# A PSUM tile of its own for each prompt head's scores, and another place for the second gate's weights, in a two-layer hybrid decoder step

## The chip, the cores and the metric

The kernel runs on one core of a Trainium2 chip. The metric is the time of one launch in device microseconds (us), the median of the runs. Engines are named as the profile names them: PE is TensorE's matmul, PEld its weight load, DVE VectorE, ACT ScalarE, POOL GpSimd, SP SyncE, which here only issues DMAs.

## What is computed

Two layers work on a prompt of 256 tokens and on 8 samples of 8 tokens (320 tokens together). Each layer adds to x the output projection of three gated branches: a pooling mixer, latent attention (MLA) and a gated delta rule. One projection of the normalised x feeds all of them and the gates. The change lies in the latent attention of the prompt:

```python
def _mla_attend(q_lat, q_rope, c_kv, k_rope, q_pos, k_pos):
...
        s = (jnp.einsum('bqhc,bkc->bhqk', ql, c_kv, preferred_element_type=jnp.float32)
             + jnp.einsum('bqhr,bkr->bhqk', qr, k_rope, preferred_element_type=jnp.float32)) * MLA_SCALE
        mask = k_pos[None, :] <= qp[:, None]
        p = jax.nn.softmax(jnp.where(mask[None, None], s, -jnp.inf), axis=-1)
        o = jnp.einsum('bhqk,bkc->bqhc', p.astype(c_kv.dtype), c_kv, preferred_element_type=jnp.float32)
```

There are 8 heads. The gates are `sigmoid` of columns of the same input projection and scale each branch's product with its output weights.

## The kernel before

A layer runs in this order: projections with the pooling and the delta rule (a scheduler sets the order of the instructions there, by its own estimate of times), then the **head stage** (latent attention of the prompt, head by head), then the **sample stage** (the 8 samples' attention over 2048 cached tokens each, one sample at a time), then the branch products and the output projection. In the head stage and the sample stage the order on PE, DVE, ACT and POOL is the order in which the code is written (`manual_schedule`); each of these engines does its instructions in that order, and one that waits holds up all behind it.

The head stage is a loop over h = 0 to 10, which has several heads under way at once. In round h:

- **scores** of head h (L1278, L1279): four products on PE into 384 columns of a PSUM bank; `head_max` (L1283, L1284): two maxima on DVE; `head_soften` (L1289, L1290): two exponentials on ACT with their sums;
- for h < 2 the **values** (L1358), 4 products; for h = 4 the POOL queue gets the gather of the second sample's cache;
- a **flip** (L1167, L1164) on DVE: it transposes a quarter of the first sample's keys, or its rotary part, into KT and krT. `flips` says in which round which of the five is done;
- head h - 2 is **turned** (L1301): three transposes on PE into an A tile, copied by ACT to pPT (L1303);
- in rounds 2, 3, 7 and 8 half of a **gate** product (L220 to L222): 12 products on PE;
- `head_scale` (L1294 to L1296): reciprocals of the sums on DVE, then two multiplications on POOL. The turning of the head waits for them;
- head h - 3 is **attended** (L1310, L1311) from pPT and the values; DVE puts the result into zs (L1312).

A gate's weights come by `gate_w`: a load to wraw on the SP queue, ahead by four buffers, then `split_w`, which makes two halves, wh by a copy on ACT (L196) and wl by a subtraction on DVE (L197), which waits for wh. The second gate's `gate_w` stands at the end of round 4, so that DVE meets it ahead of the maxima of head 5 (the sixth head).

The scores of all heads go into one PSUM tile, hsc, of four banks: head h uses the quarter h % 4. The framework follows what reads and writes a tile as a whole: the scores of a head wait for the exponentials of the head before (L1290). The same four banks then hold the sample scores sc (L1177), which round 9 begins; four more, the A tiles, serve the turned heads, the attended heads and the gates. Ahead of this stage the eight banks belong to another pool, in which the last users are the products kn (L1123), copied by ACT (L1125).

Of the kernel before, what the change touches and what calls it, by code (L numbers as in the profile page):

```python
# [11 lines left out]
F32 = mybir.dt.float32  # L12
# [5 lines left out]
PSUM = bass.MemoryType.PSUM  # L18
# [98 lines left out]
def trunk(tc, I, O, layers=2):  # L117
# [3 lines left out]
    pool = lambda name, **k: ctx.enter_context(tc.tile_pool(name=name, bufs=1, **k))  # L121
# [20 lines left out]
    def enter(*a, **k):  # L142
        st = ExitStack()
        return st, st.enter_context(phase(*a, **k))
# [265 lines left out]
    for l in range(layers):  # L410
# [717 lines left out]
        p1c.close()  # L1128
        kvp = p2c.enter_context(tc.tile_pool(name=f"kv_{l}", bufs=1, side="right", reuse_waits="tile"))
        olat = p2.tile([128, 2, 8, 64], F32, tag="qlat", name="olat", bufs=1)  # L1130
        p2b, pa = enter(f"pa_{l}", dict(A=4, S=1), "right")
        pdc, phc, pbc = ExitStack(), ExitStack(), ExitStack()
        pd = pdc.enter_context(tc.tile_pool(name=f"pd_{l}", bufs=1, reuse_waits="tile"))

        def load_wuv(t):
# [33 lines left out]
        def scores(keys, q4):  # L1169

            KT, krT = keys
            sc = banks["pool"].tile([128, 4, 512], F32, tag="S", name="sc", bufs=1)
            for k in range(9):
                for hf in range(2):
                    for g in range(4):
                        r, keys_ = slice(32 * g, 32 * g + 32), slice(256 * hf, 256 * hf + 256)
                        nc.tensor.matmul(  # L1177
                            sc[64 * hf : 64 * hf + 64, g, :256], q4[r, k, :], krT[r, keys_] if k == 8 else KT[r, k, keys_],
                            start=k == 0, stop=k == 8,
                        )  # L1180
            return sc
# [160 lines left out]
        with tc.manual_schedule(engines={mybir.EngineType.PE, mybir.EngineType.DVE, mybir.EngineType.Activation, mybir.EngineType.Pool}):  # L1342
            ph = phc.enter_context(tc.tile_pool(name=f"ph_{l}", bufs=1, side="right", reuse_waits="tile"))
            wuv = load_wuv(ph.tile([128, 1024], F32, name="wuv"))
            vv = ph.tile([128, 2, 512], F32, name="vv")

            im = ph.tile([128, 2, 128], F32R, name="im")
            act(im[:, 0], ident, AF.Copy)
            act(im[:, 1], c("causal")[:, :128], AF.Copy)
            gather(0)  # L1350
            q4 = load_q(0)
            nm, w = gate_w()
            hsc = banks["pool"].tile([128, 4, 512], F32, tag="S", name="hsc", bufs=1)

            def values(t):
                b = ps("A", "vv")
                for cc in range(2):
                    nc.tensor.matmul(b, ckv[:, cc, t * 128 : t * 128 + 128], wuv[:, cc, :], start=cc == 0, stop=cc == 1)  # L1358
                act(vv[:, t, :], b, AF.Copy)


            keys = key_tiles()
            flips = {3: 0, 4: 1, 5: 2, 6: 3, 7: 4}
            hs, hp = {}, {}
            b = sc = None
            for h in range(11):
                if h < 8:
                    head_scores(h, hsc[:, h % 4])
                    st2 = head_max(hsc[:, h % 4])
                    hs[h] = head_soften(hsc[:, h % 4], st2), st2  # L1370
                if h < 2:
                    values(h)
                if h == 4:
                    gather(1)
                if h in flips:
                    flip(0, keys, flips[h])
                if h - 2 in hs:
                    hp[h - 2] = head_turned(hs[h - 2][0])
                if h in (2, 3):
                    b = gate_mm("A", w, b, (4 * (h - 2), 4 * (h - 2) + 4))  # L1380
                if h in (7, 8):
                    b = gate_mm("A", w, b, (4 * (h - 7), 4 * (h - 7) + 4))
                if h in hs:
                    head_scale(*hs[h])
                if h - 3 in hs:
                    head_attend(h - 3, hp[h - 3])
                if h == 3:
                    gate_out(nm, b, True)
                    b = None
                if h == 4:  # L1390
                    nm, w = gate_w()
                if h == 8:
                    gate_out(nm, b, True)
                    pair[0] = paired[0] = 1
                    gs = [gate_w() for _ in range(GL[0])]
                if h == 9:
                    sc = scores(keys, q4)
            phc.close()
            pb = pbc.enter_context(tc.tile_pool(name=f"pb_{l}", bufs=1, side="right", reuse_waits="tile"))
            q4 = load_q(1)  # L1400
            mx = stats(0)
            o = None
            for bb in range(NB):
                more = bb + 1 < NB
                S = soften(bb, sc, mx)
                if more:
                    keys = key_tiles()
                    flip(bb + 1, keys, 0)
                    nmx = stats(bb + 1)
                softened(bb, S, mx)  # L1410
                if more:
                    flip(bb + 1, keys, 1)
                g = [(gs[0][0], gate_mm("A", gs[0][1]))]
                if o is not None:
                    ob = combine(o)
                    combined(bb - 1, ob)
                gate_out(*g[0], bb < 6)
                if more:
                    flip(bb + 1, keys, 4)
                    flip(bb + 1, keys, 2)  # L1420
                two = len(gs) > 1
                if two:
                    b = gate_mm("A", gs[1][1], ks=(0, 4))
                PT = turned_p(S)
                PTn = turned_own(bb)
                if two:
                    gate_mm("A", gs[1][1], b, (4, 8))
                    gate_out(gs[1][0], b, bb < 6)
                weigh(bb, mx)
                o = attend(bb, PT, PTn, mx)  # L1430
                if more:
                    flip(bb + 1, keys, 3)
                    gs = [gate_w() for _ in range(GL[bb + 1])]
                    sc = scores(keys, q4)
                    mx = nmx
                    if bb + 2 < NB:
                        q4 = load_q(bb + 2)
            wuv = load_wuv(pb.tile([128, 1024], F32, tag="S", name="wuv", bufs=2))
            pdc.close()
            p3e = ExitStack()  # L1440
            p3a = p3e.enter_context(tc.tile_pool(name=f"p3a_{l}", bufs=1, reuse_waits="tile"))
            yb = {}
            split_y(p3a, 0)
# [10 lines left out]
                    nc.tensor.matmul(b[64 * e : 64 * e + 64, p * 64 : p * 64 + 64], wuv[:, cc, h * 64 : h * 64 + 64], olat[:, cc, h, :], start=cc == 0, stop=cc == 1)  # L1454
        for p in range(4):
            stt(zs[4 + p][:, TP:], b[:, p * 64 : p * 64 + 64], 0.5, zs[4 + p][:, TP:], mult, mult)
        pbc.close()
        p2b.close()
        p2c.close()
# [90 lines left out]
```

## Time and profile before

| | |
|---|---|
| median of 3 runs | 1057.81 us (1056.7 to 1057.89) |
| profiled execution | 1062.18 us |
| its span | 1060.1 us |
| mean granted clock of PE in it | 0.968 |
| PE busy | 995.1 us, 94% of the span |
| DVE busy | 708.6 us, 67% |
| ACT busy | 465.0 us, 44% |
| POOL busy | 329.5 us, 31% |

The span is what the profile shows of the launch; the profiled execution is 4.4 us longer than the median. The granted clock is a share of TensorE's full speed: at 1 it runs at 2.4 GHz, at 0.5 at 1.2 GHz. "Busy" counts neither DMA issue nor waiting. PE is the engine that is busy most, so what matters is where PE waits, for whom, and where it runs at the lower clock.

### The profile page before, as it was taken

The numbers are of one execution on the slowest core, as the hardware profiler recorded it, in microseconds if no ns is written. First come the engines' busy times: TensorE is split into PE (matmuls) and PEld (weight loads), VectorE is DVE, ScalarE is ACT, GpSimd is POOL, SyncE is SP. The second block draws the span as 40 slices with busy tenths as digits, with TensorE's granted clock in tenths as the row PEclk, the third lists the DMA queues.
The fourth block names the chain that finished last, engine by engine and source line by source line (L and its number), as shares of the span: only waits on it lengthen the run. The fifth ranks groups of instructions, "written<-read, shape, count | busy, mean of one in ns | idle before, by whom it ended". The sixth has DMA issues, their size and how long they took to land. (4 is left out here: it accounts for less than half of the span.)

```text
span 1060.1 us, 24775 instructions
## 1 busy us (share of the span) xinstructions
PE 995.1 (94%) x10211; PEld 869.1 (82%) x10211; DVE 708.6 (67%) x1353; ACT 465.0 (44%) x838; POOL 329.5 (31%) x467
## 2 busy tenths in 40 slices
PE   8989899999989999989989978989999999999996
PEld 6877798887878887779978867979887778777996
DVE  3899984558556666568659878645674657674872
ACT  5554353454543333344546624326445333334453
POOL 3566321215240101035345542212234211000631
PEclk7999999999989999999999979999999999999998
DMA  8533333633746776258563322345264477742861
GB/s 232 154 81 99 100 84 91 182 96 113 211 131 191 245 232 228 79 166 249 141 200 82 99 80 72 99 133 133 81 161 156 150 255 220 248 156 86 262 177 50
DMA packets 202698, 159.22 MB, mean 150 GB/s; under 512 B 27704, under 2 KB 191826, under 8 KB 200010
## 3 DMA queue, kind: packets, MB, share of 16 engines
q1 hardware_dynamic: 176364, 98.47, 34.3%
q0 software_dynamic: 7424, 48.75, 12.8%
q10 hardware_dynamic: 18798, 10.44, 3.4%
q8 instruction: 80, 1.31, 0.5%
q14 instruction: 32, 0.26, 0.1%
HBM read 144.17 MB, written 13.68 MB: 149 GB/s over the span
## 5 line engine op out<-in xcount | busy, mean ns | idle before, releaser
L197 DVE TENSOR_TENSOR wl<-wraw,wh 128x1024 fp32r<-128x1024 f32 (+2 forms) x169 | 195.2, 1164 | 80.3 <-ACT wh L196 79.6
L196 ACT ACTIVATE wh<-wraw 128x1024 fp32r<-128x1024 f32 (+1 forms) x180 | 166.2, 935 | 165.2 <-PE pj L221 77.8
L220 PE MATMUL pj<-xnH,wh 128*128 128x320 f32 (+1 forms) x528 | 175.4, 332 | 16.9 <-DVE V L497 6.1
L222 PE MATMUL pj<-xnH,wl 128*128 128x320 f32 (+1 forms) x528 | 172.4, 327 | 7.4 <-DVE wl L197 7.1
L221 PE MATMUL pj<-xnL,wh 128*128 128x320 f32 (+1 forms) x528 | 170.7, 323 | 0.0
L220 PE MATMUL gate<-xnH,wh 128*128 128x320 f32 x384 | 125.1, 326 | 1.7 <-DVE V L497 1.5
L220 PEld LDWEIGHTS pj<-xnH,wh 128*128 128x128 f32 (+1 forms) x528 | 103.8, 197 | 23.3 <-ACT wh L196 8.3
L222 PE MATMUL gate<-xnH,wl 128*128 128x320 f32 x384 | 120.5, 314 | 1.6 <-DVE wl L197 1.3
L221 PE MATMUL gate<-xnL,wh 128*128 128x320 f32 x384 | 119.7, 312 | 0.0
L222 PEld LDWEIGHTS pj<-xnH,wl 128*128 128x128 f32 (+1 forms) x528 | 103.5, 196 | 11.8 <-DVE wl L197 9.1
L221 PEld LDWEIGHTS pj<-xnL,wh 128*128 128x128 f32 (+1 forms) x528 | 103.7, 196 | 5.2 <-issue 3.8
L220 PEld LDWEIGHTS gate<-xnH,wh 128*128 128x128 f32 x384 | 72.9, 190 | 9.3 <-issue 5.7
L1167 DVE STREAM_TRANSPOSE KT<-kv 128x1024 f32<-128x1024 f32 x64 | 78.6, 1228 | 0.4
L222 PEld LDWEIGHTS gate<-xnH,wl 128*128 128x128 f32 x384 | 72.7, 189 | 3.0 <-DVE wl L197 1.8
L221 PEld LDWEIGHTS gate<-xnL,wh 128*128 128x128 f32 x384 | 73.0, 190 | 1.0 <-issue 0.8
L220 PE MATMUL br<-yH,wh 128*128 128x320 f32 x192 | 59.7, 314 | 5.2 <-ACT wh L196 3.3
L1248 PE MATMUL pv<-kv,PT 128*64 128x256 f32 x512 | 58.8, 382 | 2.3 <-ACT PT L1226 2.3
L1177 PE MATMUL sc<-KT,q 32*64 32x256 f32 x2048 | 59.3, 377 | 0.0
L221 PE MATMUL br<-yL,wh 128*128 128x320 f32 x192 | 59.1, 309 | 0.0
L222 PE MATMUL br<-yH,wl 128*128 128x320 f32 x192 | 58.4, 309 | 0.0
L505 DVE SCALAR_TENSOR_TENSOR cy<-V,prm,cy 128x344 f32<-128x344 f32 x72 | 56.4, 803 | 0.5
L1177 PEld LDWEIGHTS sc<-KT,q 32*64 32x64 f32 x2048 | 45.8, 131 | 12.0 <-issue 5.7
(410 smaller groups left out, 2046.8 us busy)
## 6 DMA issues: line engine op xcount, KB each, us to landing
wraw<-in_w_in SPq DMA_DIRECT2D x114, 512.0 KB
wraw<-in_w_out SPq DMA_DIRECT2D x16, 512.0 KB
q<-q4d SPq DMA_DIRECT2D x64, 72.0 KB
gate<-gt ACTq DMA_DIRECT2D x28, 160.0 KB
gt<-gate POOLq DMA_DIRECT2D x28, 160.0 KB, 3.7
wraw<-in_w_br_pool SPq DMA_DIRECT2D x16, 256.0 KB
wraw<-in_w_br_dn SPq DMA_DIRECT2D x16, 256.0 KB
wraw<-in_w_br_mla SPq DMA_DIRECT2D x16, 256.0 KB
```

The costliest lines, as they stand in the source:

```text
L196: act(h, raw, AF.Copy)
L197: (nc.gpsimd.tensor_tensor if spare or turn[0] in K["lo"] else tt)(lo, raw, h.bitcast(F32), sub)
L220: nc.tensor.matmul(out, wh[:, k, :], xh[:, first + k, :], start=k == 0, stop=False)
L221: nc.tensor.matmul(out, wh[:, k, :], xl[:, first + k, :], start=False, stop=False)
L222: nc.tensor.matmul(out, wl[:, k, :], xh[:, first + k, :], start=False, stop=k == nk - 1)
L505: stt(y, V[:, j : j + 344], wj(j), y, mult, add)
L1167: nc.vector.transpose(v[:, a], kv[:, a * 1024 : a * 1024 + 1024].rearrange("p (i k c) -> p i k c", i=4, k=8))
L1177: nc.tensor.matmul(sc[64 * hf : 64 * hf + 64, g, :256], q4[r, k, :], krT[r, keys_] if k == 8 else KT[r, k, keys_], start=k == 0, stop=k == 8,)
L1248: nc.tensor.matmul(pv[64 * hf : 64 * hf + 64, :256], PT[:, n * 128 + 64 * hf : n * 128 + 64 * hf + 64], kv[:, r : r + 256], start=n == 0, ...
```

## The change

Each head's scores get a tile of one bank (tag H, four buffers) in a PSUM pool of their own, hp. The pool is closed in round 9, and the sample scores get another, sp, which is closed after the sample stage. The pool pa keeps the A tiles alone. The second gate's `gate_w` moves from the end of round 4 into round 5, behind the maxima and exponentials of head 5. Flips 2, 3 and 4 move from rounds 5, 6 and 7 to rounds 6, 7 and 8.

```diff
--- before.py
+++ after.py
@@ -1128,8 +1128,9 @@
         p1c.close()
         kvp = p2c.enter_context(tc.tile_pool(name=f"kv_{l}", bufs=1, side="right", reuse_waits="tile"))
         olat = p2.tile([128, 2, 8, 64], F32, tag="qlat", name="olat", bufs=1)
-        p2b, pa = enter(f"pa_{l}", dict(A=4, S=1), "right")
-        pdc, phc, pbc = ExitStack(), ExitStack(), ExitStack()
+        p2b, pa = enter(f"pa_{l}", dict(A=4), "right")
+        pdc, phc, pbc, hpc, spc = (ExitStack() for _ in range(5))
+        bank4 = lambda st, name: st.enter_context(tc.tile_pool(name=f"{name}_{l}", bufs=1, space=PSUM, reuse_waits="tile"))
         pd = pdc.enter_context(tc.tile_pool(name=f"pd_{l}", bufs=1, reuse_waits="tile"))
 
         def load_wuv(t):
@@ -1169,7 +1170,7 @@
         def scores(keys, q4):
 
             KT, krT = keys
-            sc = banks["pool"].tile([128, 4, 512], F32, tag="S", name="sc", bufs=1)
+            sc = sp.tile([128, 4, 512], F32, tag="S", name="sc", bufs=1)
             for k in range(9):
                 for hf in range(2):
                     for g in range(4):
@@ -1350,7 +1351,7 @@
             gather(0)
             q4 = load_q(0)
             nm, w = gate_w()
-            hsc = banks["pool"].tile([128, 4, 512], F32, tag="S", name="hsc", bufs=1)
+            hp_ = bank4(hpc, "hp")
 
             def values(t):
                 b = ps("A", "vv")
@@ -1360,18 +1361,21 @@
 
 
             keys = key_tiles()
-            flips = {3: 0, 4: 1, 5: 2, 6: 3, 7: 4}
+            flips = {3: 0, 4: 1, 6: 2, 7: 3, 8: 4}
             hs, hp = {}, {}
             b = sc = None
             for h in range(11):
                 if h < 8:
-                    head_scores(h, hsc[:, h % 4])
-                    st2 = head_max(hsc[:, h % 4])
-                    hs[h] = head_soften(hsc[:, h % 4], st2), st2
+                    hsc = hp_.tile([128, 512], F32, tag="H", name="hsc", bufs=4)
+                    head_scores(h, hsc)
+                    st2 = head_max(hsc)
+                    hs[h] = head_soften(hsc, st2), st2
                 if h < 2:
                     values(h)
                 if h == 4:
                     gather(1)
+                if h == 5:
+                    nm, w = gate_w()
                 if h in flips:
                     flip(0, keys, flips[h])
                 if h - 2 in hs:
@@ -1387,13 +1391,13 @@
                 if h == 3:
                     gate_out(nm, b, True)
                     b = None
-                if h == 4:
-                    nm, w = gate_w()
                 if h == 8:
                     gate_out(nm, b, True)
                     pair[0] = paired[0] = 1
                     gs = [gate_w() for _ in range(GL[0])]
                 if h == 9:
+                    hpc.close()
+                    sp = bank4(spc, "sp")
                     sc = scores(keys, q4)
             phc.close()
             pb = pbc.enter_context(tc.tile_pool(name=f"pb_{l}", bufs=1, side="right", reuse_waits="tile"))
@@ -1454,6 +1458,7 @@
                     nc.tensor.matmul(b[64 * e : 64 * e + 64, p * 64 : p * 64 + 64], wuv[:, cc, h * 64 : h * 64 + 64], olat[:, cc, h, :], start=cc == 0, stop=cc == 1)
         for p in range(4):
             stt(zs[4 + p][:, TP:], b[:, p * 64 : p * 64 + 64], 0.5, zs[4 + p][:, TP:], mult, mult)
+        spc.close()
         pbc.close()
         p2b.close()
         p2c.close()
```

On PE in the head stage of layer 0 these are the rows from head 5's scores to the start of head 6's, with the semaphores that each waits for (named by the engine that raises them); first before, then changed (line numbers are one higher there):

```order
L1278 MATMUL hsc<-kn,qx_2283 128x128 [waits Activation_49]
L1279 MATMUL hsc<-im 128x128
L1278 MATMUL hsc<-kn,qx_2283 128x256
L1279 MATMUL hsc<-im 128x128
L1301 MATMUL pT<-cst,pS 128x128 [waits DVE_49,Pool_49]
L1301 MATMUL pT<-cst,pS 128x128 [waits Pool_49]
L1301 MATMUL pT<-cst,pS 128x128
L1310 MATMUL po<-pPT,vv 64x256 [waits DVE_49,Activation_49]
L1311 MATMUL po<-pPT,vv 64x128
L1278 MATMUL hsc<-kn,qx_2282 128x128 [waits Activation_49]
L1279 MATMUL hsc<-im 128x128
```

And the same place in the changed kernel:

```order
L1279 MATMUL hsc<-kn,qx_2283 128x128
L1280 MATMUL hsc<-im 128x128
L1279 MATMUL hsc<-kn,qx_2283 128x256
L1280 MATMUL hsc<-im 128x128
L1302 MATMUL pT<-cst,pS 128x128 [waits DVE_49,Pool_49]
L1302 MATMUL pT<-cst,pS 128x128 [waits Pool_49]
L1302 MATMUL pT<-cst,pS 128x128
L1311 MATMUL po<-pPT,vv 64x256 [waits DVE_49,Activation_49]
L1312 MATMUL po<-pPT,vv 64x128
L1279 MATMUL hsc<-kn,qx_2282 128x128
L1280 MATMUL hsc<-im 128x128
```

The order is the same; the waits of the scores for ACT are gone, those of the turned and the attended head stand.

On DVE in the head stage of layer 0, from the weights of the second gate on, first before, then changed (L1283 and L1284 are maxima, L1167 a flip, L1294 the reciprocals, L1312 a result; wl is the weight half):

```order
L1167 STREAM_TRANSPOSE KT<-kv 128x4x8x32
L1294 RECIPROCAL st_3512<-st_3512 128x2
L1312 SCALAR_TENSOR_TENSOR zs<-po,zs 64x256
L197 TENSOR_TENSOR wl<-wraw,wh 128x1024
L1283 TENSOR_REDUCE st_3546<-hsc 128x1
L1284 TENSOR_REDUCE st_3546<-hsc 128x1
L1167 STREAM_TRANSPOSE KT<-kv 128x4x8x32
L1294 RECIPROCAL st_3546<-st_3546 128x2
L1312 SCALAR_TENSOR_TENSOR zs<-po,zs 64x256
L1283 TENSOR_REDUCE st_3570<-hsc 128x1
```

And the same place in the changed kernel:

```order
L1168 STREAM_TRANSPOSE KT<-kv 128x4x8x32
L1295 RECIPROCAL st_3519<-st_3519 128x2
L1313 SCALAR_TENSOR_TENSOR zs<-po,zs 64x256
L1284 TENSOR_REDUCE st_3548<-hsc 128x1
L1285 TENSOR_REDUCE st_3548<-hsc 128x1
L197 TENSOR_TENSOR wl<-wraw,wh 128x1024
L1295 RECIPROCAL st_3548<-st_3548 128x2
L1313 SCALAR_TENSOR_TENSOR zs<-po,zs 64x256
L1284 TENSOR_REDUCE st_3578<-hsc 128x1
L1285 TENSOR_REDUCE st_3578<-hsc 128x1
L1168 STREAM_TRANSPOSE KT<-kv 128x4x8x32
```

The weight half moved behind two maxima, and ahead of the reciprocal of the same head; the flip of that round moved on to the next.

The scheduler sets the projections' order by its own estimate, and that came out otherwise in layer 1, in two places. This is DVE at one of them, the triangular inversion (R and X are its recursion, TS its result; z, wl and th belong to a projection), first before, then changed:

```order
L761 TENSOR_TENSOR X_7149<-X_7149,a_6588 128x20x6
L654 TENSOR_TENSOR z<-pj,rn 128x320
L762 TENSOR_TENSOR R<-R,X_7149 128x20x6
L760 STREAM_SHUFFLE X_7153<-R 128x160
L197 TENSOR_TENSOR wl<-wraw,wh 128x1024
L761 TENSOR_TENSOR X_7153<-X_7153,a_6588 128x20x7
L657 SCALAR_TENSOR_TENSOR th<-th,z 128x320
L762 TENSOR_TENSOR R<-R,X_7153 128x20x7
L768 TENSOR_TENSOR TS<-R,cst_6398 128x512 x2
L768 TENSOR_TENSOR TS<-R,cst_6398 128x256
```

And the same place in the changed kernel:

```order
L761 TENSOR_TENSOR X_7164<-X_7164,a_6603 128x20x6
L762 TENSOR_TENSOR R<-R,X_7164 128x20x6
L760 STREAM_SHUFFLE X_7168<-R 128x160
L761 TENSOR_TENSOR X_7168<-X_7168,a_6603 128x20x7
L762 TENSOR_TENSOR R<-R,X_7168 128x20x7
L654 TENSOR_TENSOR z<-pj,rn 128x320
L768 TENSOR_TENSOR TS<-R,cst_6413 128x512 x2
L768 TENSOR_TENSOR TS<-R,cst_6413 128x256
L197 TENSOR_TENSOR wl<-wraw,wh 128x1024
L657 SCALAR_TENSOR_TENSOR th<-th,z 128x320
```

The projection's steps z, wl and th moved from between the steps of the recursion to behind it.

## Rows read from the trace of the kernel before

**Rows 1.** PE's waits in the whole span: total us, times, longest us.
```profile
PE pj L222 <- DVE wl L197: 7.1, 6, 2.5
...
PE hsc L1278 <- ACT pS L1290: 5.4, 4, 2.0
...
PE hsc L1278 <- ACT kn L1125: 0.9, 1, 0.9
```

**Rows 2.** Timeline, layer 0's head stage: start us, us, engine, line, operation [idle before <- releaser].
```profile
286.21 1.63 ACT L1125 ACTIVATE kn<-kn 64x256 f32<-64x256 f32 x4 [0.36 <-PE kn L1123]
...
286.88 0.39 PE L1278 MATMUL hsc<-kn,qx 96*128 96x128 f32 x2
...
301.15 0.38 PE L1311 MATMUL po<-pPT,vv 128*64 128x128 f32 x2
...
302.21 0.49 PE L1278 MATMUL hsc<-kn,qx 128*128 128x128 f32 x2 [0.68 <-ACT pS L1290]
302.38 0.43 DVE L1312 SCALAR_TENSOR_TENSOR zs<-po,zs 64x256 f32<-64x256 f32 x1
302.42 1.07 ACT L196 ACTIVATE wh<-wraw 128x1024 fp32r<-128x1024 f32 x1
...
303.52 1.22 DVE L197 TENSOR_TENSOR wl<-wraw,wh 128x1024 fp32r<-128x1024 f32 x1 [0.70 <-ACT wh L196]
...
304.77 0.29 DVE L1283 TENSOR_REDUCE st<-hsc 128x1 f32<-128x128 f32 x1
...
306.32 0.49 ACT L1303 ACTIVATE pPT<-pT 128x384 f32<-128x384 f32 x1
306.47 0.15 DVE L1294 RECIPROCAL st<-st 128x2 f32<-128x2 f32 x1
...
306.48 0.79 PE L1278 MATMUL hsc<-kn,qx 96*128 96x128 f32 x2 [2.05 <-ACT pS L1290]
306.54 0.40 DVE L1312 SCALAR_TENSOR_TENSOR zs<-po,zs 64x256 f32<-64x256 f32 x1
306.72 0.60 POOL L1295 TENSOR_SCALAR pS<-pS,st 128x128 f32<-128x128 f32 x1 [2.76 <-DVE st L1294]
...
307.30 0.92 POOL L1296 TENSOR_SCALAR pS<-pS,st 128x256 f32<-128x256 f32 x1
...
320.02 3.71 PE L1177 MATMUL sc<-KT,q 32*64 32x256 f32 x128
```

**Rows 3.** Timeline of layer 1's head stage, the same columns.
```profile
805.10 0.49 PE L1278 MATMUL hsc<-kn,qx 96*128 96x128 f32 x2 [0.86 <-ACT kn L1125]
...
806.23 0.29 DVE L1283 TENSOR_REDUCE st<-hsc 128x1 f32<-128x128 f32 x1 [4.32 <-PE hsc L1279]
...
824.70 0.15 DVE L1294 RECIPROCAL st<-st 128x2 f32<-128x2 f32 x1
...
829.36 0.49 PE L1301 MATMUL pT<-cst,pS 128*128 128x128 f32 x3
...
829.61 0.39 PE L220 MATMUL gate<-xnH,wh 128*128 128x320 f32 x1
...
836.65 3.71 PE L1177 MATMUL sc<-KT,q 32*64 32x256 f32 x128
```

**Rows 4.** Windows around the waits: stretch, us, busy of each engine, granted clock, DMA.
```profile
302.20:306.48 4.28, 2.22 (x14) 1.60 (x14) 3.51 (x8) 2.25 (x7) 1.68 (x3) 1.00 0.77 318
306.48:313.30 6.82, 6.82 (x24) 5.41 (x25) 3.45 (x11) 1.63 (x7) 3.00 (x4) 0.50 0.58 209
...
824.70:828.70 4.00, 3.99 (x16) 2.77 (x16) 2.68 (x8) 1.62 (x6) 1.99 (x3) 0.57 0.84 293
```

**Rows 5.** Windows of layer 0's sample stage and of layer 1's projections.
```profile
324.90:420.00 95.10, 95.10 (x1261) 79.30 (x1262) 64.05 (x120) 33.27 (x63) 13.22 (x23) 1.00 0.71 230
...
620.00:720.00 100.00, 87.83 (x1174) 80.02 (x1172) 67.69 (x141) 34.64 (x55) 26.62 (x39) 0.95 0.37 99
```

## The prediction

> **What bounds the kernel now.** I read the list of what TensorE (PE) waited for first. One entry names the tile of this change: PE stood before the score products of a prompt head (L1278) until an exponential of the head before (L1290) was done, 5.4 us in 4 waits, the longest 2.0 [rows 1]. That is two waits in each layer. Next I read the timeline of the head stage in layer 0, where the reader is to see the two waits: 0.68 us before head 5 and 2.05 us before head 6 [rows 2]. The scores of heads 5 and 6 go into banks that ScalarE isn't reading; the wait is there because all four banks are one tile. Third, the windows: right after the second wait PE's granted clock is 0.50, which is the lower of its two levels, 1.2 instead of 2.4 GHz, for 6.82 us in layer 0, and 0.57 on average over 4.00 us in layer 1; in the stretch before, PE was busy 2.22 of 4.28 us [rows 4]. The wait thus costs twice. Last, the window of the sample attention that follows: PE busy 95.10 of 95.10 us [rows 5]. So what the head stage ends earlier is not waited away there.
>
> **The change, part by part.** The order of PE's instructions in the head stage is the same. What is different: seven waits for the exponentials are gone in each layer, VectorE does the sixth head's two maxima ahead of the gate's weight half wl, ScalarE the two exponentials ahead of wh, one flip sits one head later three times, and the banks of the A tiles and of the scores have changed places.
>
> *Heads 1 to 4* gain nothing. Their waits for the exponential lie beside products already under way (values, gate halves); the list has only two PE waits per layer.
>
> *Heads 5 to 7, layer 0.* With the wait gone PE is no longer the follower of the exponential, so I follow what is late next.
> (a) Scores of head 5 can begin when head 1's attend product ends: 301.15 + 0.38 = 301.53 instead of 302.21.
> (b) Maxima: 1.13 us after the scores begin (805.10 to 806.23, [rows 3]), 302.66; VectorE is busy with head 1's result until 302.38 + 0.43 = 302.81. Take 302.8. Before it was 304.77, behind wl.
> (c) The exponentials are over 1.55 us after the maxima begin (304.77 to 306.32, where the next copy begins): 304.35.
> (d) ScalarE then does wh, and VectorE's wl begins 1.10 us after wh (302.42 to 303.52): 305.45. Behind wl on VectorE, which waits for wh, now stand the reciprocal of head 5, the result of head 2 and the maxima of head 6.
> (e) What follows wl begins 1.25 us after it (303.52 to 304.77): reciprocal of head 5 at 306.70. Before: 306.47. So the weights are the new stop, and this reciprocal is 0.2 us later, not earlier.
> (f) GpSimd scales head 5's weights: from 0.25 us after the reciprocal (306.47 to 306.72) to 307.30 + 0.92 = 308.22, that is 1.75 after it: 308.45.
> (g) In the meantime PE has done heads 6 and 7's scores. Scores of 6 follow at once; the copy that head 3's attend product needs begins 1.07 us after wh began (302.42 + 1.07 in its row), 305.4, and takes 0.49, so that product starts at 306.0; scores of 7 are done by 307.7. PE waits about 1.1 and 0.7 us here, in place of 0.68 and 2.05, and then turns head 5's weights when (f) is done. From turning to the gate products are 0.25 us (829.36 to 829.61, [rows 3]): the gate begins at 308.7.
> (h) From there to the sample scores nothing is late: heads 6 and 7 have their maxima at 307.2 and 309.5, by the steps above (1.70 us from maxima to reciprocal, then 0.4 for the result), and are turned only after half a gate each, at about 311 and 314. The stretch took 836.65 - 829.61 = 7.04 us at full clock in layer 1 [rows 3], so the sample scores begin at 315.75 instead of 320.02 [rows 2]. **Gain 4.27 us**, if the clock doesn't fall.
>
> *Layer 1.* Reciprocal of head 5 there at 824.70, 518.23 later than in layer 0. By the same steps the gate begins at 826.9 instead of 829.61: **gain 2.68 us**. Layer 0 gains more because its low clock lasted longer.
>
> *The first head's bank.* In layer 1 head 0's scores waited 0.86 us for the last copies of kn [rows 1, 3]; in the changed program they wait for nothing there: gain 0.86. In layer 0 they now wait, for the copies of the third kn product: its two copies are half of a row of four that begins at 286.21 and takes 1.63, so 287.0 against a start at 286.88 [rows 2]; between 0 and, for all four copies, 1.0 us; I take 0.3, nearest to the half. Together **gain 0.56**.
>
> *Flips and pools.* Flips 2 to 4 begin one head later. Each ran under an exponential and does so again; the last (0.7 us) is done by about 313, and the sample scores come at 315.7, so they cost nothing; without that cover one would cost its length. The GpSimd order and the order on the DMA queues of SP and GpSimd are the same. The pool sp closes ahead of pb and adds no work.
>
> *The second layer's order.* Outside of the head stage the scheduler put a few projection products and VectorE steps of layer 1 in another order, at two places (the triangular inversion, and the products U and W). No row shows the new order. PE idles 12.17 of 100 us in that stretch [rows 5]; the longest single wait for weights of the whole trace is 2.5 us [rows 1]. I bound each place by one such wait gained or lost, 3.5 us for both if they are independent, and take zero, since the order shown has VectorE's inversion ahead of a gate in one place and the weights later in another.
>
> The sum: 4.27 + 2.68 + 0.56 = **7.5 us**. The profiled execution took 1062.18 us, its span 1060.1; so 1054.7 for such a one. The median of the runs is 1057.81, 4.4 below it, and the same saving gives **1050.3**.
>
> **A rule weighed.** The rows show a PE that was busy 2.22 of 4.28 us and then ran at the lower level, for longer in layer 0 than in layer 1 although both run the same instructions [rows 4]. The Trainium skill, "TensorE: Matmul & The Clock Gate", section "What's actually happening", says that a block sets the clock by how busy PE has been recently, and that it runs freely and doesn't restart with the kernel. The trace agrees as far as the two lengths go. By that rule the fall may come back with the 1.1 and 0.7 us of idle time that remain, which is the first rival below.
>
> **The rivals.** *The clock still falls* behind the two remaining waits. For: 1.8 us of idle time in 4 us are not far from the 2.06 that came before the fall [rows 4]. Against: it is less, and in two pieces. Until 308.4 the low clock would hide under GpSimd's scaling. After that, if it lasts 3.4 us from 306.5 (half of layer 0's 6.82), 1.5 us of work run at half speed: 0.75 us lost; if it lasts 6.8, 4.9 us do: 2.45. One of each: 3.2 us, gain 4.3, **1053.5** (1051.8 to 1055.2).
> *The next stage takes it back*: the sample stage is held by transfers, so that it starts and ends when it did. For: it moves 230 GB/s at a DMA share of 0.71. Against: PE has no idle time in it at all [rows 5], so no transfer ends late there, and the head stage's own weights come four tiles ahead. Then 1057.8, no change.
> *Slower: the second layer's order.* The new order there puts PE behind VectorE in the inversion. Each displaced group can cost a wait like the 2.5 us one; from four of them on (10 us) the 7.5 us are lost, and with five (12.5) it is **1062.8**. Against: PE idles only 12.17 us in the whole stretch [rows 5], so this would have to double it.
> *It doesn't do what it says*: excluded; the changed program's PE rows have no wait for the exponential.
>
> **How the numbers follow.** Forecast 1050.3: 0.62, its own range 1046.8 to 1053.8 by the 3.5 us. Clock still falls: 0.22. Taken back: 0.09. Slower: 0.07. The range takes in the first two, 1046.8 to 1055.2; outside lie 0.16 and a little of the tails. A measurement of this kernel can tell about 0.2%, 2.1 us, from no change. Faster 0.62 + 0.22 + 0.01 = 0.85; same 0.08; slower 0.07.
>
> **What would show it.** In the profile after: the list of PE's waits has no entry of scores for the exponentials; wl begins near 305.4 and the reciprocal of head 5 near 306.7; the gate products begin near 308.7 and the sample scores near 315.7 (layer 1: from score to score of the two kinds, 28.9 us instead of 31.55); the granted clock stays at 1 in the window from head 6 on; head 0 of layer 1 starts without a wait. It would be wrong if wl came much later than 305.4 (wh late), if the clock fell as before, or if the second layer's stretch between its start and the head stage grew or shrank by over 3.5 us.

## The result, and the profile after

The changed kernel took 1045.15 us (median of 4, 1043.93 to 1047.41) against 1057.58 for the kernel before (median of 4): ratio 0.988, 95% interval 0.985 to 0.991. That is 12.4 us less where 7.5 were forecast, and 1.65 us below the lower end of the range. Two more groups of runs gave 0.990 (0.987 to 0.993) and 0.990 (0.987 to 0.994). Single executions of one kernel spread far more than the three known beforehand: 31 of the kernel before, in one group, lay between 1051.45 and 1066.38. Executions more than 1.5% above the fastest of their kernel are left out of ratios and medians here; that concerns two of tiles_only, at 1062.95 and 1063.09.

The page of the profile after, and its granted clock in 40 slices of the span:

```profile
span 1042.6 us, 24784 instructions
...
PE 986.0 (95%) x10211; PEld 863.6 (83%) x10211; DVE 710.1 (68%) x1353; ACT 465.4 (45%) x838; POOL 330.0 (32%) x467
...
PEclk7989999999999999999999989999999999999998
```

The same clock line of the kernel before:

```profile
PEclk7999999999989999999999979999999999999998
```

The first 8 of before's line (slice 12, from 291.5 us) is the fall in layer 0's head stage; after has none there. In the list of PE's waits the 5.4 us for the exponentials [rows 1] are gone; two new entries from the same stage stand in it (total us, times, longest us):

```profile
PE po L1311 <- ACT pPT L1304: 1.7, 2, 0.8
...
PE pT L1302 <- POOL pS L1297: 1.1, 2, 0.6
```

Timeline of after in layer 0's head stage, heads 5 and 6, columns as in [rows 2]:

```profile
300.75 0.49 PE L1279 MATMUL hsc<-kn,qx 128*128 128x128 f32 x2
...
302.13 0.29 DVE L1284 TENSOR_REDUCE st<-hsc 128x1 f32<-128x128 f32 x1
...
303.68 1.05 ACT L196 ACTIVATE wh<-wraw 128x1024 fp32r<-128x1024 f32 x1
...
304.76 1.23 DVE L197 TENSOR_TENSOR wl<-wraw,wh 128x1024 fp32r<-128x1024 f32 x1 [2.01 <-ACT wh L196]
305.17 0.65 PE L1311 MATMUL po<-pPT,vv 128*64 128x256 f32 x2 [0.84 <-ACT pPT L1304]
...
305.91 0.16 DVE L1295 RECIPROCAL st<-st 128x2 f32<-128x2 f32 x1
...
306.81 0.93 POOL L1297 TENSOR_SCALAR pS<-pS,st 128x256 f32<-128x256 f32 x1
...
307.79 0.44 PE L1302 MATMUL pT<-cst,pS 128*128 128x128 f32 x2 [0.57 <-POOL pS L1297]
...
307.99 0.39 PE L220 MATMUL gate<-xnH,wh 128*128 128x320 f32 x1
...
315.02 0.47 PE L1178 MATMUL sc<-KT,q 32*64 32x256 f32 x8
```

Scores, maxima, wh, wl, reciprocal, gate: the order the prediction wrote down. The windows [rows 4] asked about, at the same times in after, of the engines PE's busy time alone: clock 1.00 in both instead of 1.00 and 0.50.

```profile
302.20:306.48 4.28, 3.44 (x21) 1.00 0.93 392
306.48:313.30 6.82, 6.25 (x40) 1.00 0.47 157
```

To see where 17.5 us of span went between the two profiles, I divided each trace at the starts of products that every version has: the first kn product, the first sample score sc, the first wo product, and layer 1's first projection product pj, its three gates and its first kn product. The differences of these starts, for all profiles of this study that are needed below (us; "head" is first kn to first sc; "layer 1's stretch" is first pj to first kn, and its parts run from gate to gate; the rest, from gate 3 to kn, took 61.7 to 62.4 in all):

| profile | head, layer 0 | sc to wo, layer 0 | stretch | pj to gate 1 | 1 to 2 | 2 to 3 | head, layer 1 |
|---|---|---|---|---|---|---|---|
| before | 36.96 | 181.34 | 268.55 | 60.03 | 89.45 | 57.35 | 36.39 |
| before_again | 35.40 | 181.59 | 270.94 | 60.74 | 88.38 | 59.79 | 35.57 |
| layer1_only | 35.44 | 180.91 | 265.67 | 59.42 | 85.56 | 58.96 | 32.18 |
| tiles_only | 32.57 | 181.27 | 265.20 | 60.44 | 85.20 | 57.84 | 32.31 |
| old_order | 32.57 | 181.07 | 265.60 | 60.55 | 85.04 | 57.59 | 32.14 |
| layer0_only | 32.42 | 182.00 | 260.61 | 59.16 | 83.64 | 56.09 | 37.96 |
| order_only | 35.54 | 181.24 | 261.36 | 60.80 | 83.65 | 55.19 | 36.46 |
| after | 32.43 | 182.16 | 259.92 | 59.38 | 83.61 | 55.22 | 32.16 |
| after_again | 32.42 | 182.58 | 260.80 | 60.24 | 83.62 | 55.22 | 32.16 |
| after_third | 32.42 | 181.75 | 261.29 | 59.22 | 83.63 | 56.05 | 32.16 |

From before to after: head stages 4.5 and 4.2 us shorter, layer 1's stretch 8.6, 0.8 given back between sc and wo; the other 1.0 lies ahead of the first kn and in layer 1's sample stage and branch products. The head stages are near what was forecast. The stretch isn't: the change touches nothing in it except the order in which the scheduler puts its instructions.

### The profile page after: what moved, and what is told of

Its sections match the earlier page's. It is cut to its first block, busy times and chain, and to the rows that moved or that the text cites. A ratio compares the mean times of both kernels' runs of the same rounds, so it can differ in the third digit from the quotient of the medians.

```text
span 1042.6 us, 24784 instructions
## 1 busy us (share of the span) xinstructions
PE 986.0 (95%) x10211; PEld 863.6 (83%) x10211; DVE 710.1 (68%) x1353; ACT 465.4 (45%) x838; POOL 330.0 (32%) x467
## 4 chain that ended last, share of the span: by engine, by line
PE 70%; DVE 15%; ACT 6%; DMA 4%; issue 3%; ACTq 1%; POOL 1%; SPq 0%; DVEq 0%; POOLq 0%
PE sc L1178 6%; PE pv L1249 6%; PE gate L220 5%; PE gate L222 5%; PE gate L221 5%; PE pj L220 5%; PE pj L222 4%; DVE cy L505 4%; PE pj L221 4%; DVE wl L197 3%; PE br L220 2%; PE br L222 2%; PE br L221 2%; PE wo L220 2%; PE wo L222 2%
## 5 line engine op out<-in xcount | busy, mean ns | idle before, releaser
L197 DVE TENSOR_TENSOR wl<-wraw,wh 128x1024 fp32r<-128x1024 f32 (+2 forms) x169 | 198.7, 1185 | 83.0 <-ACT wh L196 82.1
L220 PE MATMUL pj<-xnH,wh 128*128 128x320 f32 (+1 forms) x528 | 173.3, 328 | 14.4 <-DVE V L497 6.2
L222 PE MATMUL pj<-xnH,wl 128*128 128x320 f32 (+1 forms) x528 | 170.3, 323 | 6.7 <-DVE wl L197 6.3
```

Source lines behind the costliest of these rows:

```text
L197: (nc.gpsimd.tensor_tensor if spare or turn[0] in K["lo"] else tt)(lo, raw, h.bitcast(F32), sub)
L220: nc.tensor.matmul(out, wh[:, k, :], xh[:, first + k, :], start=k == 0, stop=False)
L222: nc.tensor.matmul(out, wl[:, k, :], xh[:, first + k, :], start=False, stop=k == nk - 1)
```

## The experiments

One program holds both versions, chosen layer by layer by three flags: TILES (four score tiles or one), GMOVE (the second gate's weights after head 5 or head 4), FMOVE (flips 2 to 4 one head later or not). The changed kernel is (1, 1) in all three. Layer 1's products have the old order when layer 0's weights stay where they were, and the new one when they move there (more orders below). On PE, ACT and POOL the instructions of the stretch stand in one and the same order in all five profiles that are called old, and in all five that are called new.

**The kernel before, again, and its layers apart.**

```diff
-TILES, GMOVE, FMOVE = (1, 1), (1, 1), (1, 1)
+TILES, GMOVE, FMOVE = (0, 0), (0, 0), (0, 0)   before_again
+TILES, GMOVE, FMOVE = (1, 0), (1, 0), (1, 0)   layer0_only
+TILES, GMOVE, FMOVE = (0, 1), (0, 1), (0, 1)   layer1_only
+TILES, GMOVE, FMOVE = (1, 1), (0, 0), (0, 0)   tiles_only
```

The texts of this group count layer 1's stretch from the first oml product, 75 us ahead of pj; so counted it took 346.1, 336.1, 340.1 and 340.0 us in the order of the list. Theory A is the one that is called theory O further down.

> The kernel before once more, with a new profile. The stretch from the end of layer 0's sample stage (first product into oml, L1454) to the first kn product of layer 1 took 343.4 us in the first profile of before and 335.6 in the profile of the change. Theory A (the changed order of layer 1's projections is worth several us): about 340 to 343 here. Rival B (the 7.8 us are chance, where the clock happened to fall in one execution): 336 to 339. Time: 1057.6 us by both.

Measured: 1059.17, ratio 1.002 (0.999 to 1.005); stretch 270.94, so the long stretch is no accident of the first profile; it is 3 us above what theory A gave. Its head stages were 35.40 and 35.57, up to 1.6 shorter than in the first profile: the cost of the low clock varies.

> Own tiles, moved weights and moved flips in layer 0 alone; layer 1's head stage as before. The scheduler then gives layer 1's projections the order that they have in the change. Theory A: 4.5 us from layer 0's head stage and 3.5 us or more from the order, 1049.5 us, and the stretch from oml to kn near 336. Rival B (the order is worth nothing): 1053 us, stretch as in before_again.

Measured: 1051.31, ratio 0.994 (0.992 to 0.997). The stretch is 260.61, as theory A says, though layer 1's code is the old one. The median lies between A's 1049.5 and B's 1053 and doesn't part them. Its unchanged head stage in layer 1 took 37.96, the longest of all, behind the same 2.0 us wait:

```profile
PE hsc L1280 <- ACT pS L1292: 2.7, 2, 2.0
```

```profile
812.00:824.70 12.70, 12.70 (x67) 0.77 0.21 68
```

The first is its list of waits, the second a window after that wait: clock 0.77 on average over 12.7 us in which PE never stood. The clock was at 0.50 in the first half of it (to 817.8).

> The same change in layer 1 alone; layer 0 and the order of all projections as before. Theory A: 4.2 us from layer 1's head stage and nothing else, 1053.4 us, the stretch from oml to kn as in before_again. Rival B: 1053.4 us as well, but then layer0_only has the same time; if the shares of the two layers don't sum to the whole change, they depend on each other.

Measured: 1054.99, ratio 0.998 (0.995 to 1.000); stretch 265.67; head stage 32.18. The stretch is the old order's, as theory A says, and among its shorter ones: 5 us below that of before_again, which has the same order. The median is 2.1 below the kernel before instead of 4.2, and the interval takes in no change. The two layers apart give 5.8 and 2.1 us, together 8.0, where the whole gives 10.7 to 12.4; the intervals, 2.9 to 8.9 and -0.2 to 5.0, are too wide to say whether the layers depend on each other.

> A tile for each head's scores in both layers, but the second gate's weights and the flips where they were; the order on every engine is that of before, projections too. My sum: head 5's reciprocal stays at 306.5, its turning ends near 308.5, PE waits some 2 us for the copy of head 3 and the clock may fall there; gain 4.0 and 3.5 us if it does not, 1050 us, and 2 us less per layer if it does, 1054. Rival C (without moved weights the tiles are worth nothing, since the maxima still wait behind wl): 1056 to 1057.6.

Measured: 1052.44 (median of ten, 1047.22 to 1057.27), ratio 0.995 (0.992 to 0.998). Its head stages are 32.57 and 32.31, so rival C falls: in the profile the tiles alone give all but 0.15 us in each stage of what tiles and moves give. The timeline of tiles_only at the place of the one of after above:

```profile
302.66 1.23 DVE L198 TENSOR_TENSOR wl<-wraw,wh 128x1024 fp32r<-128x1024 f32 x1 [0.70 <-ACT wh L197]
...
303.92 0.29 DVE L1285 TENSOR_REDUCE st<-hsc 128x1 f32<-128x128 f32 x1
...
306.01 0.65 PE L1312 MATMUL po<-pPT,vv 128*64 128x256 f32 x2 [1.82 <-ACT pPT L1305]
...
307.98 0.39 PE L221 MATMUL gate<-xnH,wh 128*128 128x320 f32 x1
```

wl stands 2.1 us earlier and head 5's maxima 1.8 later than in after, PE waits 1.82 in one piece instead of 0.84 and 0.57, and the gate starts at the same time. The clock stayed at 1.00 in this execution. Whether it does in all of them after a wait of 1.82 isn't shown; the median is 2.8 us above the profiled execution (1049.69).

**The order alone, and the same head stages with the old order.**

```diff
-TILES, GMOVE, FMOVE = (1, 1), (1, 1), (1, 1)
+TILES, GMOVE, FMOVE = (0, 0), (1, 0), (0, 0)   order_only
+TILES, GMOVE, FMOVE = (1, 1), (0, 1), (0, 1)   old_order
```

after_again and after_third are the changed kernel.

> One score tile in both layers as before, flips as before; only layer 0's second gate weights come after head 5 instead of head 4, which gives layer 1 the changed kernel's order of projection products. Theory O: layer 1's stretch 259 to 262 us instead of 265 to 271; layer 1's head stage 35.4 to 38.0 as before; layer 0's between 33 and 37; median 1049 to 1053 against 1057. Rival R: stretch 265 to 271, median 1055 to 1057.

> The changed kernel once more, beside the others of this group. So far the head stage (first kn product to first sample score) took 35.4 to 38.0 us in five profiled stages with one score tile and 32.2 to 32.6 in six with four tiles; layer 1's stretch from its first projection product to its first kn product took 265 to 271 us in four profiles with the old order of its products and 260 to 261 in two with the new. Theory O (the new order is worth about 6 us by itself, beside about 7.5 from two head stages): stretch 259 to 262, median 1043 to 1047, ratio to before 0.986 to 0.990. Rival R (the short stretches were chance, the change is its head stages): stretch 264 to 271, median 1049 to 1051, ratio 0.992 to 0.994.

Measured: order_only 1054.38, ratio 0.997 (0.994 to 0.999), with a stretch of 261.36 and head stages as long as those of before (35.54, 36.46). In layer 0 that is another stage than before's: the moved weights put a wait of 3.06 us ahead of head 7's scores, and the clock stayed at 1.00. after_again 1046.69, stretch 260.80. Both stretches as theory O says; order_only's median is 1.4 us above what it gave and 0.6 below what rival R gave, so it doesn't decide.

> The changed kernel, but in layer 0 the gate's weights and the flips stand where they stood before; that alone leaves layer 1's projection products in the old order. Both head stages: 32.2 to 32.6 us, as with the tiles alone and with the whole change. So this kernel and the changed one, on one chip in one group, differ by the order alone. Theory O (the order is worth 5 to 7 us): layer 1's stretch 264 to 271, median 1050 to 1054, 5 to 8 us above the changed kernel's. Rival R (the stretches of single profiles are chance: weights_after_head5 and weights_within_head6 have the same order and 268.8 and 258.0): median within 3 us of the changed kernel's.

> The changed kernel once more, beside old_order. Theory O: layer 1's stretch 259 to 262, median 1044 to 1047. Rival R: stretch anywhere from 258 to 269, median within 3 us of old_order's.

Measured, side by side on one chip: old_order 1051.56 (1048.62 to 1059.12), after_third 1046.13 (1045.33 to 1049.65), 5.4 us apart with head stages equal to 0.15 us. Theory O holds and rival R falls. (old_order's layer 0 has the 1.82 us wait of tiles_only, so that a part of the 5.4 may be falls of the clock there, in executions without a profile. The two profiled executions, without such a fall, are 4.5 apart, and their stretches 4.3.) Over all profiles, five with either order: from gate 1 to 2 the old order took 85.04 to 89.45 us (mean 86.73), the new one 83.61 to 83.65; from gate 2 to 3 57.35 to 59.79 (58.31) against 55.19 to 56.09 (55.55). Together 5.9 us. The stretch as a whole spreads by more than that even in one order: moves_only, weights_after_head5 and weights_within_head6 below share a fourth, and took 262.31, 268.81 and 257.99.

What the order does is seen in PE's timeline. old_order, the triangular inversion (Y), then the products around U and W:

```profile
632.00 0.41 PE L221 MATMUL pj<-xnH,wh 128*128 128x320 f32 x1 [1.00 <-ACT wh L197]
632.25 0.31 PE L222 MATMUL pj<-xnL,wh 128*128 128x320 f32 x1
633.42 1.00 PE L794 MATMUL Y<-TS,ATm 64*64 64x32 f32 x28 [0.87 <-DVE TS L771]
...
643.89 0.41 PE L221 MATMUL pj<-xnH,wh 128*128 128x320 f32 x1 [0.16 <-DVE z L655]
...
688.02 1.15 PE L847 MATMUL ktv<-cst,co 64*64 64x64 f32 x32 [0.84 <-ACT ktv L865]
...
703.32 0.41 PE L221 MATMUL pj<-xnH,wh 128*128 128x320 f32 x1 [1.10 <-ACT wh L197]
...
704.58 0.41 PE L223 MATMUL pj<-xnH,wl 128*128 128x320 f32 x1 [0.70 <-DVE wl L198]
```

after_third, the inversion (around U and W it has none of these three waits):

```profile
629.85 1.82 PE L794 MATMUL Y<-TS,ATm 64*64 64x32 f32 x56 [1.15 <-DVE TS L771]
...
636.37 0.78 PE L648 MATMUL mix<-d,mixw 128*128 128x320 f32 x2 [0.31 <-DVE d L646]
...
640.26 0.41 PE L221 MATMUL pj<-xnH,wh 128*128 128x320 f32 x1 [0.75 <-DVE z L655]
```

And a window behind the Y products in each, first old_order, then after_third:

```profile
636.00:639.00 3.00, 3.00 (x12) 0.50 0.65 175
```

```profile
632.50:636.00 3.50, 3.50 (x33) 1.00 0.55 150
```

In the old order two projection products stand ahead of Y, and the first waits 1.00 us for its weights; then Y waits 0.87, and PE's clock falls to 0.50, the level of 1.2 GHz, for 3 us. In the new one these two products stand behind Y, and the clock doesn't fall there. The waits shown are no shorter, 2.21 us (1.15, 0.31 and 0.75) instead of 2.03 (1.00, 0.87 and 0.16), so what went here in this pair is the low clock. In the ten profiles PE stood from gate 1 to gate 2 for 8.72 to 11.62 us in the old order (mean 10.07) and 8.77 to 9.72 in the new (9.24), 0.8 of the 3.1 us by which the means of this part differ; in each of the five old ones the clock fell within 10 us of Y's start, in none of the five new ones did it fall between there and gate 2. Around U and W three waits of 2.64 us together are gone. In after the first of them stays, with 0.54; in after_third PE ran at a clock of 0.50 just ahead of it (681.1 to 684.5), and likewise in layer0_only: in these two the part took 56.05 and 56.09, in the other three of the new order 55.19 to 55.22.

**The moves without the tiles, and the tiles without the flips.**

```diff
-TILES, GMOVE, FMOVE = (1, 1), (1, 1), (1, 1)
+TILES, GMOVE, FMOVE = (0, 0), (1, 1), (1, 1)   moves_only
+TILES, GMOVE, FMOVE = (1, 1), (1, 1), (0, 0)   tiles_and_gate
```

> One score tile as before, but the gate's weights and the flips moved in both layers. By the steps of the prediction head 5's scores still wait 0.68 us; the maxima then come ahead of wl, the exponentials are over near 304.9, and head 6's scores wait for them until then instead of 306.48, so that the gate begins near 309.3: head stage 33 to 34 us if TensorE's clock doesn't fall, 35 if it does. Rival: without tiles of their own the heads wait for each other as before, stage 35.4 to 38. Layer 1's products stand in a fourth order, stretch 256 to 272 by theory O. Median 1046 to 1060.

Measured: 1051.44, ratio 0.994 (0.991 to 0.997); head stages 34.41 and 35.43, stretch 262.31. The wait behind the weights moved on by one head, from head 6's scores to head 7's, with nearly its old size (timeline, layer 0):

```profile
300.74 0.49 PE L1280 MATMUL hsc<-kn,qx 96*128 96x128 f32 x2 [0.67 <-ACT pS L1292]
...
304.88 0.49 PE L1280 MATMUL hsc<-kn,qx 128*128 128x128 f32 x2 [1.92 <-ACT pS L1292]
```

The expectation's steps up to head 6 were right; that head 7 waits next was overlooked. Layer 1's stage lies at the lower end of what the rival gave (35.4 to 38). Much of the 6 us of this run lies in the stretch again.

> The change without its move of the flips. This gives layer 1's projection products a third order. Both theories: head stages 32.2 to 32.7 us, since the flips run under other work. Theory O: the time then differs from the changed kernel's only by the stretch of the third order; I can't tell its sign: stretch 256 to 272, median 1041 to 1056, and the difference of the medians equals that of the stretches to 3 us. Rival R: stretch 264 to 271 by chance, median 1049 to 1051 as for any kernel with both head stages changed.

Measured: 1048.19, ratio 0.990 (0.987 to 0.993); stretch 261.72 with the third order. But the head stages were 33.56 and 34.79, not 32.2 to 32.7. The flip (L1169) stood ahead of head 5's reciprocal:

```profile
305.03 1.24 DVE L1169 STREAM_TRANSPOSE KT<-kv 128x1024 f32<-128x1024 f32 x1
...
306.19 0.12 DVE L1296 RECIPROCAL st<-st 128x2 f32<-128x2 f32 x1
...
307.14 0.33 PE L1303 MATMUL pT<-cst,pS 128*128 128x128 f32 x1 [0.96 <-POOL pS L1297]
```

The flip takes 1.24 us behind wl, and what waits for it is a chain: reciprocal, scaling, turning, gate. In layer 1 the same waits in the same order were followed by a fall, which layer 0 didn't have (window of layer 1's gate):

```profile
815.60:819.00 3.40, 3.40 (x14) 0.52 0.08 20
```

**A place for the weights that leaves PE no wait.** In after, two waits (0.84 and 0.57) remain in each head stage. Two other places of the gate's weights:

```diff
                     st2 = head_max(hsc)
+                    if h == 6:
+                        nm, w = gate_w()        weights_within_head6
                     hs[h] = head_soften(hsc, st2), st2
...
-                if h == 5:
-                    nm, w = gate_w()
...
                     head_attend(h - 3, hp[h - 3])
+                if h == 5:
+                    nm, w = gate_w()            weights_after_head5
```

weights_within_head6 has flips {3: 0, 4: 1, 5: 2, 7: 3, 8: 4} besides.

> The changed kernel with the gate's weights at the end of head 5's part instead of ahead of its flip: ScalarE does head 3's copy before wh, VectorE head 5's reciprocal before wl. In the changed kernel PE waits 0.84 us (head 3's attend product, for its copy behind wh) and 0.57 us (head 5's turning, for GpSimd's scaling) in each layer. Theory P (these two waits are the weights', but the whole is held by a chain): both waits vanish and the gate starts 1.4 us earlier, near 306.6 by layer 0's clock of the profile of after, but head 6's maxima still stand behind wl (306.5), so that its scaling ends near 310 and PE waits about 1.5 us ahead of turning head 6, between the gate's halves: head stage 32.0 to 32.6, as in the changed kernel (32.2 to 32.4). Rival Q (the two waits were PE's loss): stage 31.0 (32.4 less 1.4). Layer 1's products stand in the order of moves_only (its stretch was 262.3). Median 1045 to 1050.

Measured: head stages 31.40 and 31.13, nearer to rival Q's 31.0 than to theory P's 32.0 to 32.6; the gate starts 23.65 us after the first kn product (25.40 in after), and one wait of 0.29 us is left before head 6 is turned, not the 1.5 expected: between the gate's halves PE also has head 4's attend product to do, and the sum had left it out. Median 1045.26, ratio 0.990 (0.988 to 0.992), though the profiled execution (1050.19) was the longest of its six; its stretch of 268.81 belongs to that.

> The changed kernel with the gate's weights between head 6's maxima and its exponentials, and the third flip back at head 5: ScalarE does wh after head 3's copy and before head 6's exponentials, VectorE head 6's maxima before wl. By theory P all of the waits go: head 5's scaling ends near 305.7, the gate starts near 306.5 with wl done at 306.5, head 6's scaling ends near 308.3 when the gate's first half does. Head stage 30.8 to 31.3 us in each layer, 1.1 to 1.6 less than in the changed kernel; the list of PE's waits has no or less than 0.3 us of entries for head 3's copy and head 5's scaling. Rival: a wait of the same size appears elsewhere in the stage (head 7's turning, or the gate for wl), stage 32.0 to 32.6. Layer 1's products as in moves_only: stretch 260 to 263. Median 1042 to 1047 (rival 1045 to 1050).

Measured: head stages 30.68 and 30.42, no PE wait at all. The windows from the first head's scores to sc, layer 0 and layer 1:

```profile
285.50:312.20 26.70, 26.70 (x157) 1.00 0.57 188
786.50:813.10 26.60, 26.60 (x157) 1.00 0.57 189
```

and of after:

```profile
286.56:315.02 28.46, 27.04 (x157) 1.00 0.54 176
791.27:819.61 28.34, 26.94 (x158) 1.00 0.52 177
```

PE is now busy 26.70 of 26.70 us there, so no wait is left in this stage; it takes 3.5 us less than after in both layers together. Median 1044.16 (1038.12 to 1051.19), ratio 0.991 (0.987 to 0.994): the lowest median here, but its interval doesn't part it from the changed kernel's, and its stretch (257.99 in the profile) has the fourth order, the one of moves_only and weights_after_head5. That the shorter head stages make the whole faster than the changed kernel isn't shown.

## Why the prediction was wrong, point by point

**The step that failed is "The second layer's order"**, taken as 0 with 3.5 us either way. It measured 5.4 us between old_order and after_third, 5.9 (gate 1 to gate 3) between the means of five profiles each, and 3.0 (0.8 to 5.9) for order_only against the kernel before. The prediction had named this sign itself: a stretch that changes by over 3.5 us. For one place 2.5 us was not far off, the means by place are 3.1 and 2.8; but both places gained, and neither by one such wait. At the inversion PE stood only 0.8 us less; the falls of the clock behind Y went, and the low clock wasn't priced there, although it was in the head stage: [rows 5] shows 0.95 as the mean clock of that window. At U and W two or three waits went, none of them the longest of the trace: a bound by the longest single wait isn't a bound on their sum. The sign could have been asked: which of the moved products had waited in the trace of before. The rival "slower by the second layer's order" had the right place with the wrong sign.

**The head stages were sized nearly right in sum, 7.5 us, but not layer by layer.** By all the profiled stages of the table: layer 0 with one tile and nothing moved 36.96, 35.40 and 35.44 (mean 35.93) against 32.42 or 32.43 in four with the whole change, so 3.5; layer 1 36.39, 35.57, 37.96 and 36.46 (mean 36.60) against 32.14 to 32.18 in five, 4.4. Together 7.9. The prediction's terms, with the first head's bank, are 4.0 for layer 0 and 3.5 for layer 1; it gave layer 0 more for its longer low clock, and over several profiles it is layer 1 that gains more. That the two misses cancel is luck.

**Steps (a) to (h)** hit nearly to a constant. Predicted and measured: scores of head 5 301.53 and 300.75, maxima 302.8 and 302.13, wl 305.45 and 304.76, reciprocal 306.70 and 305.91, gate 308.7 and 307.99, sc 315.75 and 315.02. All are 0.67 to 0.79 early, and that gap stands already at (a): 0.32 because head 0 began at 286.56 instead of 286.88, as the first kn product had come earlier; the rest on heads 1 to 4, which the prediction gave nothing. In layer 1 score to score took 28.34 where 28.9 was forecast. The two waits forecast as 1.1 and 0.7 are 0.84 and 0.57.

**The moved weights earn next to nothing in the head stage.** tiles_only reaches the gate at the same time without them, in the profiled execution. There the tiles do it; the move of the weights, in layer 0, matters because it gives layer 1 another order.

**Flips.** Costing nothing is right where the change puts them. The prediction named an exponential as the cover of each and worked it out for the last alone; tiles_and_gate shows the price of the third (head 5's) without cover, 1.1 us, near its length of 1.24, and, with the clock, 2.6.

**The first head's bank.** Layer 1: no wait, as said. Layer 0: kn to first score 3.97 instead of 3.82, so 0.15 lost, where 0.3 was taken.

**The rivals.** The clock didn't fall behind the two waits in four stages of layer 0 and five of layer 1 with the whole change. It fell in one of tiles_and_gate's with 2.36 us of waits. The rule weighed, the Trainium skill, "TensorE: Matmul & The Clock Gate", section "What's actually happening", that the monitor of PE's activity runs freely, fits its two stages: 1.00 in layer 0, 0.52 in layer 1, behind the same waits. No run here varies that by itself. Taken back by the next stage: hardly. sc to wo in layer 0 is 0.2 to 1.7 longer where the whole change is in layer 0 (181.75 to 182.58, against 180.91 to 181.59), and part of it is a fall in the branch products behind a wait of 1.92 us that both orders have. Window of those products, old_order and then after:

```profile
448.27:459.00 10.73, 8.81 (x80) 1.00 0.36 112
```

```profile
448.29:459.00 10.71, 8.79 (x71) 0.86 0.36 103
```

The clock fell there in all four profiles with the whole change in layer 0, and in one of the other six, before_again (458.8 to 462.2). Why stays open; so does what in the scheduler turns a move in layer 0 into another order in layer 1. The parts, 7.9 and 3 to 6, less about 0.8, give 10 to 13 us; the three groups measured 12.4, 10.7 and 11.2.

## What to carry over

A change to one stage can be worth as much through the order that it gives another stage as through itself: compare the order of the whole program, look in the trace for the waits of each product that moved, and price their sum and the clock after them, not one wait. Test a change's parts one by one: here the part that was argued step by step (the weights) earned next to nothing in its own stage. When a wait remains behind weights that two engines must prepare, look at where they lie in both queues: between the maxima and the exponentials of head 6 (with the third flip at head 5) the stage has no wait of PE; it is 0.7 us longer in each layer with the weights a step earlier, 1.7 with two.

## What the runs showed of the hardware

One kernel on one chip spreads over 10 us and more (kernel before, 31 runs, 1051.45 to 1066.38; moves_only, 12 runs, 1045.14 to 1060.77), and the profiles show one place of it. The same instructions behind the same wait of 2.05 us were followed by 6.82 us at a clock of 0.50 in layer 0 of before, by 4 us at 0.57 in its layer 1 [rows 4], and by 11 us at 1.00 in layer 1 of before_again:

```profile
824.44:835.50 11.06, 10.39 (x64) 8.23 (x64) 5.57 (x15) 3.54 (x13) 4.60 (x8) 1.00 0.30 104
```

The unchanged head stage took 35.40 to 37.96 us, the twelve stages of the table with tiles, in which the clock didn't fall, 32.14 to 32.57. Another order of products can take such falls away with little of the waits: gate 1 to gate 2 took 83.61 to 83.65 us in five profiles of the new order, 85.04 to 89.45 in five of the old, 3.1 less on average, while PE stood only 0.8 less. So a removed wait or another order can be worth more than the waits that went, by an amount that one profile doesn't tell: the same stage of the kernel before took 35.40 and 36.96 us.
